# Block products of the merge gates: weight sums by accumulating DMAs, activation sums and one conditioning group in other stages

## The chip, the core and the metric

One core of a Trainium2 chip runs the whole program. The metric is the device time of one execution in microseconds; of the kernel before three executions were timed, and their median stands for it.

## The reference

Two layers of a trunk with 512 latent and 128 context tokens, which the kernel runs as one block of 640 tokens (5 tiles of 128) with 1024 channels. Cut to what matters here:

```python
def _layer(x, shift, scale, gate, w_in_l, conv_w_l, w_branch_l, w_o_l, ln_g_l, ln_b_l, attn_fn):
    h = (_layernorm(x) * (1.0 + scale) + shift).astype(x.dtype)
    q, k, v, z_a, cb, cc, cx, z_b, fx, z_c, g = jnp.split(h @ w_in_l, offsets, axis=-1)
    y_a = attn_fn(q, k, v) * jax.nn.silu(z_a)
    y_b = _short_conv(cb, cc, cx, conv_w_l) * jax.nn.silu(z_b)
    y_c = _fourier(fx) * jax.nn.silu(z_c)
    gates = jax.nn.sigmoid(g.reshape(b, s, N_BRANCH, D_MODEL))
    merged = (gates[:, :, 0] * (y_a @ w_branch_l[0]) + gates[:, :, 1] * (y_b @ w_branch_l[1])
              + gates[:, :, 2] * (y_c @ w_branch_l[2]))
    r = _layernorm(DEEPNORM_ALPHA * x + gate * (merged @ w_o_l)) * ln_g_l + ln_b_l
```

`shift`, `scale` and `gate` come from silu(cond) @ w_mod + b_mod. Everything is float32.

## The kernel before

Every matrix product is made of three matmuls: each operand is split into a high and a low part (ScalarE copies the high part, `copy`; VectorE or GpSimd subtracts for the low part), and high x high, high x low and low x high are added up in PSUM. Weights come through `Raw.load` (SP's DMA queue, 256 KB each, 6 buffers of the pool `wr`) and are split into `hl` tiles (5 buffers of `wp`). The lists of `Load(raws, steps)` in the order of the jobs set the order of loads, sums and splits; `run` emits them as far ahead as 6 raw and 5 split tiles allow, and a scheduler then orders the instructions of each engine, which run in order.

A layer goes: keys, values and queries; attention with the other projections as filler; the Fourier branch (`use_fx`, `channels`, `positions`, between the projections of `fx` and `z_c`); the gate stage; the output projection. The first layer also computes the conditioning of the second: group (1, 1) in `mod_steps` beside the Fourier stage, with loads `modf` of 256 KB, and groups (1, 2) and (1, 3) as `mod_piece`s (loads `rawm` of 512 KB, products and sums `moda` on VectorE), one after each pair of the gate stage.

The gate stage computes the 3072 gate columns. Twelve times a layer, `pair(b, m)` takes two blocks of 128 columns, cuts weights and activations in 2 x 2 blocks and uses seven block products in place of eight (`seventh`, 12 matmuls of 320 columns each). In the pair's four weight blocks a11, a12, a21, a22 and their sums, `Sum` makes the sums on VectorE (`sub`, three tiles and a scratch tile `s3`). The products are called p1 to p7 after the number given to `hl`; p1 and p2 need activations as they are, p5, p6, p7 the sums `T` made by `sums(q)` (q = 0, 1), and p4 needs `last_sum`, which overwrites a part of `act` once the last projection of the old activations is done. They add up in three PSUM banks y, x, z, drawn with the Fourier stage's g1, g2 and f1 to f3 from the four `aux` buffers. Between the products stand the branch products `pb` of the pair before (`between`), 24 matmuls each, in eight of the twelve pairs.

Of the kernel before, what the change touches and what calls it, by code (L numbers as in the profile page):

```python
# [19 lines left out]
TOK = 640  # L20
# [14 lines left out]
def body(nc, tc, I, O, ctx):  # L35
# [4 lines left out]
    big = pool("big", 1)  # L40
# [30 lines left out]
    def sub(out, a, b):  # L71
        nc.vector.tensor_tensor(out=out, in0=a, in1=b, op=ALU.subtract)  # L72
# [4 lines left out]
    def add(out, a, b):  # L77
        nc.vector.tensor_tensor(out=out, in0=a, in1=b, op=ALU.add)
# [46 lines left out]
    class Raw:  # L125
        def __init__(self, src, nm):
            self.src, self.nm, self.tile = src, nm, None
            self.stage = build_stage[0]

        def load(self):  # L130
            self.tile = wr.tile([128, 512], F32, name=f"raw{self.nm}", tag="raw")
            if self.src is not None:
                nc.sync.dma_start(out=self.tile, in_=self.src)

    class Split:
        def __init__(self, raw, nm, frees):
# [5 lines left out]
            copy(self.hl[:, 0], raw)  # L142
            eng.tensor_tensor(out=self.hl[:, 1], in0=raw, in1=fr(self.hl[:, 0]), op=ALU.subtract)  # L143

    class Sum:
        def __init__(self, out, a, b, frees=()):
            self.raws, self.frees = [out, a, b], frees

        def emit(self, eng):
            out, a, b = self.raws  # L150
            sub(out.tile, a.tile, b.tile)

    class Load:

# [26 lines left out]
    def job(body, load=None):  # L181
        jobs.append((load, body))

    def run():
        raws = [r for ld, _ in jobs if ld for r in ld.raws]
        steps = [x for ld, _ in jobs if ld for x in ld.steps]
        loaded = done = split = raw_live = hl_live = 0
        for i, (ld, bd) in enumerate(jobs):
            while i >= 3:
                if loaded < len(raws) and raws[loaded].stage <= stage[0] and raw_live < N_RAW:  # L190
                    raws[loaded].load()
                    loaded += 1
                    raw_live += 1
                    continue
                if done == len(steps):
                    break
                x = steps[done]
                if any(r.tile is None for r in x.raws):
                    break
                if isinstance(x, Sum):  # L200
                    x.emit(nc.vector)
                elif hl_live < N_HL:
                    behind = () if split == 4 or split > 7 else ("xT",) if split < 4 else ("hi", "lo")
                    with ExitStack() as st:
# [339 lines left out]
    def layer(l):  # L544
# [367 lines left out]
        def whole(out, kh, q, half):  # L912
            add(as_block(out), fr(block(kh, q, half, 0)), fr(block(kh, q, half, 1)))

        def sums(q):
            def body():
                def put(i, t):
                    hi, lo = (S["T"][i][:, z, 2 * q:2 * q + 2].rearrange("p k n -> p (k n)") for z in range(2))
                    split(hi, lo, t[:, :TOK])
                a, b, c = row(f"ta{l}{q}"), row(f"tb{l}{q}"), tmp(f"tc{l}{q}")  # L920
                whole(a, 0, q, 1)
                whole(b, 0, q, 0)
                whole(c, 1, q, 1)
                sub(b[:, :TOK], a[:, :TOK], b[:, :TOK])
                add(a[:, :TOK], c[:, :TOK], a[:, :TOK])
                add(c[:, :TOK], c[:, :TOK], b[:, :TOK])
                put(1, c)
                put(0, b)
                put(2, a)
            return body  # L930

        def last_sum():
            for q in range(2):
                a, b = row(f"td{l}{q}"), row(f"te{l}{q}")
                whole(a, 1, q, 0)
                hi, lo = (S["T"][1][:, z, 2 * q:2 * q + 2].rearrange("p k n -> p (k n)") for z in range(2))
                add(b[:, :TOK], fr(hi), fr(lo))
                sub(a[:, :TOK], a[:, :TOK], b[:, :TOK])
                split(block(0, q, 1, 0), block(0, q, 1, 1), as_block(a))

        def quarter(t, half):
            return t.rearrange("p (t h i) -> p t h i", h=2, i=64)[:, :, half]

        def pair(b, m, between=()):
            nm = f"{l}{b}{m}"
            (a11, a12), (a21, a22) = ([Raw(I["w_in"][l, C_G + b * 8 + 2 * m + i][:, h * 512:(h + 1) * 512],
                                           f"g{nm}{i}{h}") for h in range(2)] for i in range(2))
            s3 = Raw(None, f"g{nm}s")
            ps, G = {}, []

            def old(half, kh):
                return lambda k, z: act[:, :, z, 4 * kh + k, 64 * half:64 * half + 64]

            def new(i):
                return lambda k, z: S["T"][i][:, z, k]
# [27 lines left out]
            def plus(i, half):  # L983
                return lambda out: add(quarter(G[i], half), out, quarter(G[i], half))

            def sigmoid(o, i):
                nc.scalar.activation(o, i, AF.Sigmoid)

            def last_y(out):
                sigmoid(quarter(G[1], 0), out)  # L990
                sigmoid(quarter(G[1], 1), quarter(G[1], 1))

            def last_z(out):
                plus(0, 1)(out)
                sigmoid(G[0], G[0])

            def u3(out):
                keep(1, 1)(out)
                plus(1, 1)(ps["z"][:, :320].rearrange("p (t i) -> p t i", i=64))

            def hl(raw, frees, i):
                return Split(raw, f"g{nm}p{i}", frees)
            job(seventh("y", old(0, 0), True, keep(0, 0)), Load([a11, a21, a22, s3, a12], [hl(a11, [], 1)]))
            job(seventh("x", old(0, 1), True, plus(0, 0)), Load([], [hl(a12, [], 2)]))
            job(seventh("y", new(1), False, keep(0, 1)),
                Load([], [Sum(s3, a21, a11), Sum(a21, a21, a22), Sum(a11, a11, a21), hl(a11, [], 6)]))
            job(seventh("z", new(0), True, lambda out: None), Load([], [hl(a21, [a21], 5)]))
            job(seventh("y", new(2), False, u3), Load([], [hl(s3, [s3], 7)]))
            if between:
                between[0]()  # L1010
            job(seventh("y", lambda k, z: act[:, :, z, k, 64:128], False, last_y), Load([], [hl(a22, [a22], 4)]))
            job(seventh("z", old(1, 1), False, last_z), Load([], [Sum(a12, a12, a11, [a11]), hl(a12, [a12], 3)]))
            if between:
                between[1]()

        def use_p(b, c):
            def use(ps):
# [22 lines left out]
                    split(w[:, 0, 2 * q + z], w[:, 1, 2 * q + z], ld.raw(z))  # L1040
            job(body, load(I["w_o"][l, i // 2, (i % 2) * 2 + q], 2, f"o{l}{i}{q}", True))

        fm = {}

        def begin_mod():
            t = big.tile([128, 4096], F32, name="modf", tag="F")
            fm["a"] = t[:, :1024].rearrange("p (s n) -> p s n", s=2)
            fm["r"] = [t[:, 1024 + 512 * i:1536 + 512 * i] for i in range(6)]
        if l == 0:
            side.extend(mod_steps(((1, 1),), lambda: fm["a"], lambda: fm["r"]))  # L1050
            job(begin_mod)
        inproj(l, C_FX, use_fx(0))
        beside(2)
        inproj(l, C_FX + 1, use_fx(1))
        beside(2)
        for g in range(4):
            job(channels(g))
            beside(1)
            inproj(l, C_ZC + g, use_zc(g))
            if g == 3:  # L1060
                job(last_sum)
            beside(1)
            job(positions(g))
            if g < 2:
                inproj(l, C_FX + g + 2, use_fx(g + 2))
            if g == 1:
                beside(99)
                job(begin_sums)
                job(sums(0))
            if g == 2:  # L1070
                job(sums(1))

        pieces = [(1, n, kp) for n in ((2, 3) if l == 0 else (4, 5)) for kp in range(4)]

        def piece():
            if pieces:
# [240 lines left out]
```

## Time and profile before

| | us |
|---|---|
| median of 3 executions | 1269.46 |
| lowest, highest | 1268.49, 1272.26 |
| profiled execution, time | 1267.92 |
| profiled execution, span | 1266.1 |

| engine | busy, us | share of the span |
|---|---|---|
| TensorE matmul (PE) | 1226.5 | 97% |
| TensorE weight load (PEld) | 1178.1 | 93% |
| VectorE (DVE) | 950.4 | 75% |
| ScalarE (ACT) | 577.5 | 46% |
| GpSimd (POOL) | 174.1 | 14% |

The span is the time from the first to the last instruction; the time holds what lies around it as well. The page also gives the granted TensorE clock (a share of full speed) and the DMA traffic by slices of the span. The gate stage of the first layer runs from about 345 to 545 us of the span, that of the second from about 955 to 1155 us.

### The profile page before, as it was taken

To read this page: it belongs to the slowest core of one execution; us is meant where nothing else is said; L and a number is where in the kernel's file an instruction comes from. 1 tells how busy PE (TensorE), PEld (TensorE's weight loads), DVE (VectorE), ACT (ScalarE), POOL (GpSimd) and SP (SyncE) were. 2 spreads that over 40 slices of the span, in tenths; PEclk is the share of its full clock that TensorE was granted. 3 is DMA by queue.
4 is the path that set the end of the run, shared out by engine and by line. 5 is a ranking of instruction groups with operands and counts; after the bars stand their busy time and mean duration, and the time that the engine had idled before them with its cause. 6 is when DMAs were issued, how large, how long until landed. Compare 5 with 4: busy or idle time off the path is not lost.

```text
span 1266.1 us, 20852 instructions
## 1 busy us (share of the span) xinstructions
PE 1226.5 (97%) x8016; PEld 1178.1 (93%) x8016; DVE 950.4 (75%) x1710; ACT 577.5 (46%) x1113; POOL 174.1 (14%) x164
## 2 busy tenths in 40 slices
PE   6899999999989999999999999999997999999997
PEld 4699999999979999999889999999997999999986
DVE  6995686978999766678787655755579986766776
ACT  5446555554443443364244645555444444435410
POOL 3303223130000000000130233332000000000001
PEclk9999999999989999999999999999999999999999
DMA  9432132325124323234512221112312522323341
GB/s 378 170 123 68 51 104 72 100 67 175 34 85 165 100 83 102 76 121 132 222 71 72 67 68 50 60 51 76 101 39 78 177 90 84 117 60 101 116 183 50
DMA packets 61068, 131.07 MB, mean 104 GB/s; under 512 B 7144, under 2 KB 7720, under 8 KB 60712
## 3 DMA queue, kind: packets, MB, share of 16 engines
q1 hardware_dynamic: 59808, 125.35, 29.7%
q0 software_dynamic: 720, 4.10, 0.9%
q8 instruction: 63, 1.03, 0.3%
q14 instruction: 37, 0.30, 0.1%
q10 hardware_dynamic: 440, 0.30, 0.1%
HBM read 124.19 MB, written 5.52 MB: 102 GB/s over the span
## 4 chain that ended last, share of the span: by engine, by line
PE 91%; DVE 3%; DMA 3%; issue 1%; ACT 1%; POOL 0%; DVEq 0%; SPq 0%; POOLq 0%; ACTq 0%
PE y L964 13%; PE p L516 12%; PE p L518 12%; PE p L517 12%; PE z L964 6%; PE pb L516 5%; PE pb L518 5%; PE pb L517 4%; PE x L964 3%; PE o L1142 3%; PE o L1140 3%; PE o L1141 3%; PE pt L705 2%; PE s L656 2%; DMA rawm<-in_w_mod 1%; DMA raww<-in_w_in 1%
## 5 line engine op out<-in xcount | busy, mean ns | idle before, releaser
L516 PE MATMUL p<-act,hlw 128*128 128x256 f32 (+1 forms) x1024 | 321.2, 314 | 0.9 <-ACT vt L69 0.9
L518 PE MATMUL p<-act,hlw 128*128 128x256 f32 (+1 forms) x1024 | 318.4, 311 | 0.0
L517 PE MATMUL p<-act,hlw 128*128 128x256 f32 (+1 forms) x1024 | 317.4, 310 | 0.0
L516 PEld LDWEIGHTS p<-act,hlw 128*128 128x128 f32 x1024 | 193.4, 189 | 2.6 <-ACT vt L69 1.2
L517 PEld LDWEIGHTS p<-act,hlw 128*128 128x128 f32 x1024 | 192.7, 188 | 1.3
L518 PEld LDWEIGHTS p<-act,hlw 128*128 128x128 f32 x1024 | 192.7, 188 | 1.2
L687 POOL TENSOR_SCALAR P<-P,rc 128x384 f32<-128x384 f32 (+2 forms) x80 | 113.5, 1434 | 253.8 <-DVE rc L685 116.5
L69 ACT ACTIVATE hlw<-raww 128x512 fp32r<-128x512 f32 x136 | 84.8, 629 | 114.8 <-PE p L518 103.2
L143 DVE TENSOR_TENSOR hlw<-raww,hlw 128x512 fp32r<-128x512 f32 x130 | 91.3, 704 | 22.8 <-ACT hlw L69 21.1
L1140 PE MATMUL o<-wo,act 128*128 128x512 f32 (+1 forms) x168 | 63.5, 381 | 0.0
L1141 PE MATMUL o<-wo,act 128*128 128x512 f32 (+1 forms) x168 | 63.4, 379 | 0.0
L1142 PE MATMUL o<-wo,act 128*128 128x512 f32 (+1 forms) x168 | 63.3, 379 | 0.0
L312 POOL TENSOR_TENSOR rso<-rso,nhalf 128x1 f32<-128x1 f32 x10 | 14.2, 1425 | 355.6 <-DVE rso L311 355.6
L72 DVE TENSOR_TENSOR pT<-pt,pT 128x512 fp32r<-128x512 f32 x60 | 40.2, 686 | 16.2 <-ACT pT L69 16.1
L69 ACT ACTIVATE gs<-y 128x320 f32<-128x320 f32 x48 | 20.9, 435 | 68.8 <-PE y L964 65.1
L72 DVE TENSOR_TENSOR rawg<-rawg,rawg 128x512 f32<-128x512 f32 x72 | 49.5, 687 | 1.2
L69 ACT ACTIVATE pT<-pt 128x512 fp32r<-128x512 f32 x60 | 34.8, 594 | 30.9 <-PE pt L705 20.6
L143 POOL TENSOR_TENSOR hlw<-raww,hlw 128x512 fp32r<-128x512 f32 x6 | 8.5, 1425 | 260.7 <-ACT hlw L69 260.7
L659 DVE CUSTOM_DVE_ANT_0 P<-s,mask 128x384 f32<-128x384 f32 (+1 forms) x64 | 38.3, 617 | 6.1 <-PE s L656 5.9
L681 ACT ACTIVATE P<-P,nm 128x384 f32<-128x384 f32 (+1 forms) x64 | 42.1, 659 | 1.1 <-DVE es L72 0.7
L516 PE MATMUL pb<-yc,hlb 128*128 128x256 f32 (+1 forms) x128 | 40.1, 313 | 1.4 <-ACT hlb L69 1.4
L516 PE MATMUL pb<-yb,hlb 128*128 128x256 f32 (+1 forms) x128 | 40.0, 313 | 0.5 <-ACT hlb L69 0.5
(661 smaller groups left out, 2983.1 us busy)
## 6 DMA issues: line engine op xcount, KB each, us to landing
raww<-in_w_in SPq DMA_DIRECT2D x136, 256.0 KB, 2.9
rawg<-in_w_in SPq DMA_DIRECT2D x96, 256.0 KB, 3.0
rawm<-in_w_mod SPq DMA_DIRECT2D x32, 512.0 KB, 5.0
rawb<-in_w_branch SPq DMA_DIRECT2D x48, 256.0 KB, 2.8
rawo<-in_w_o SPq DMA_DIRECT2D x32, 256.0 KB, 3.1
sz<-in_w_mod SPq DMA_DIRECT2D x24, 256.0 KB, 2.9
dft<-in_dft POOLq DMA_DIRECT2D x2, 1542.0 KB, 7.3
x<-in_x SPq DMA_DIRECT2D x5, 512.0 KB, 6.1
```

What stands on the lines that cost most here:

```text
L69: nc.scalar.activation(out, in_, AF.Copy)
L72: nc.vector.tensor_tensor(out=out, in0=a, in1=b, op=ALU.subtract)
L143: eng.tensor_tensor(out=self.hl[:, 1], in0=raw, in1=fr(self.hl[:, 0]), op=ALU.subtract)
L516: nc.tensor.matmul(ps[:, a:b], lhsT=ld.w(0, k), rhs=mh, start=k == 0, stop=False)
L517: nc.tensor.matmul(ps[:, a:b], lhsT=ld.w(0, k), rhs=ml, start=False, stop=False)
L518: nc.tensor.matmul(ps[:, a:b], lhsT=ld.w(1, k), rhs=mh, start=False, stop=k == nk - 1)
L681: nc.scalar.activation(P[:, g, :W], srcs[g], AF.Exp, scale=0.125, bias=nm_[:, g:g + 1], accum_out=sm[:, g:g + 1])
L687: nc.gpsimd.tensor_scalar(out=P[:, g, :W], in0=P[:, g, :W], scalar1=rc[:, g:g + 1], scalar2=None, op0=ALU.mult)
L964: nc.tensor.matmul(out, lhsT=ld.w(z, k), rhs=moving(k, y), start=first and k == i == 0, stop=k == 3 and i == 2, skip_group_check=True)
L1140: nc.tensor.matmul(ps, lhsT=act[:, t, 0, k], rhs=w[:, 0], start=k == 0, stop=False)
L1141: nc.tensor.matmul(ps, lhsT=act[:, t, 0, k], rhs=w[:, 1], start=False, stop=False)
L1142: nc.tensor.matmul(ps, lhsT=act[:, t, 1, k], rhs=w[:, 0], start=False, stop=k == NK - 1)
```

## The change

1. The weight sums of a pair are made by DMAs that add their source to the tile they write (`Acc`, issued from GpSimd's queue): a21 += a22, a11 += a21 and a21 += a11 read the second operand from HBM again, a12 += a21 reads the tile. The signs of the seven products are turned so that only plus signs are left in the weights; the activation sums (`sums`, `last_sum`) and the sigmoids take the signs. `s3` is gone.
2. The order of the seven products is p1, p2, p5, p6, p7, p4, p3 (before p1, p2, p6, p5, p7, p4, p3), and the branch products stand after p5 and after p4.
3. `sums(0)` stands after the first `fx` projection and `sums(1)` after the first `positions`, in both layers. Before, `sums(0)` stood after `positions(1)` and `sums(1)` after `positions(2)`.
4. In the first layer conditioning group (1, 1) is no longer done beside the Fourier stage, but as four more pieces of the gate stage: twelve in place of eight.

```diff
-    class Sum:
-        def __init__(self, out, a, b, frees=()):
-            self.raws, self.frees = [out, a, b], frees
+    class Acc:
+        def __init__(self, out, src, frees=()):
+            self.out, self.src, self.frees = out, src, frees
+            self.raws = [out] + ([src] if isinstance(src, Raw) else [])

         def emit(self, eng):
-            out, a, b = self.raws
-            sub(out.tile, a.tile, b.tile)
+            src = self.src.tile if isinstance(self.src, Raw) else self.src
+            nc.gpsimd.dma_start(out=self.out.tile, in_=src, accum_op=ALU.add)
...
-                sub(b[:, :TOK], a[:, :TOK], b[:, :TOK])
-                add(a[:, :TOK], c[:, :TOK], a[:, :TOK])
-                add(c[:, :TOK], c[:, :TOK], b[:, :TOK])
+                sub(b[:, :TOK], b[:, :TOK], a[:, :TOK])
+                sub(a[:, :TOK], c[:, :TOK], a[:, :TOK])
+                minus(c[:, :TOK], c[:, :TOK], b[:, :TOK])
...
-                sub(a[:, :TOK], a[:, :TOK], b[:, :TOK])
+                minus(a[:, :TOK], b[:, :TOK], a[:, :TOK])
...
-            job(seventh("y", old(0, 0), True, keep(0, 0)), Load([a11, a21, a22, s3, a12], [hl(a11, [], 1)]))
-            job(seventh("x", old(0, 1), True, plus(0, 0)), Load([], [hl(a12, [], 2)]))
-            job(seventh("y", new(1), False, keep(0, 1)),
-                Load([], [Sum(s3, a21, a11), Sum(a21, a21, a22), Sum(a11, a11, a21), hl(a11, [], 6)]))
-            job(seventh("z", new(0), True, lambda out: None), Load([], [hl(a21, [a21], 5)]))
-            job(seventh("y", new(2), False, u3), Load([], [hl(s3, [s3], 7)]))
+            job(seventh("y", old(0, 0), True, keep(0, 0)), Load([a11, a12, a21], [hl(a11, [], 1), Acc(a21, srcs[1][1])]))
+            job(seventh("x", old(0, 1), True, plus(0, 0)), Load([a22], [Acc(a11, srcs[1][0]), hl(a12, [], 2)]))
+            job(seventh("z", new(0), True, lambda out: None), Load([], [hl(a21, [], 5), Acc(a21, srcs[0][0])]))
             if between:
                 between[0]()
+            job(seventh("y", new(1), False, keep(0, 1)), Load([], [hl(a21, [], 6), Acc(a12, a21, [a21])]))
+            job(seventh("y", new(2), False, third_y), Load([], [hl(a11, [a11], 7)]))
             job(seventh("y", lambda k, z: act[:, :, z, k, 64:128], False, last_y), Load([], [hl(a22, [a22], 4)]))
-            job(seventh("z", old(1, 1), False, last_z), Load([], [Sum(a12, a12, a11, [a11]), hl(a12, [a12], 3)]))
             if between:
                 between[1]()
+            job(seventh("z", old(1, 1), False, last_z), Load([], [hl(a12, [a12], 3)]))
...
-        if l == 0:
-            side.extend(mod_steps(((1, 1),), lambda: fm["a"], lambda: fm["r"]))
-            job(begin_mod)
         inproj(l, C_FX, use_fx(0))
-        beside(2)
+        job(begin_sums)
+        job(sums(0))
         inproj(l, C_FX + 1, use_fx(1))
...
             job(positions(g))
+            if g == 0:
+                job(sums(1))
             if g < 2:
                 inproj(l, C_FX + g + 2, use_fx(g + 2))
-            if g == 1:
-                beside(99)
-                job(begin_sums)
-                job(sums(0))
-            if g == 2:
-                job(sums(1))
...
-        pieces = [(1, n, kp) for n in ((2, 3) if l == 0 else (4, 5)) for kp in range(4)]
+        pieces = [(1, n, kp) for n in ((1, 2, 3) if l == 0 else (4, 5)) for kp in range(4)]
```

VectorE at the opening of the second layer's gate stage, around the product of the last `z_c` projection (`sgzc13`). `ta11`, `tb11` and `tc11` are rows of `sums(1)`, `tb1` and `tf1` the tiles `T`, `td` and `te` rows of `last_sum`. Before:

```order
L75 TENSOR_TENSOR sgzc13_10078<-p1_33_10029,sgzc13_10078 128x640
L143 TENSOR_TENSOR hlg110p7_10086<-rawg110s_9752,hlg110p7_10086 128x512
L72 TENSOR_TENSOR tb11_9990<-ta11_9989,tb11_9990 128x640
L72 TENSOR_TENSOR yc1_9344<-sgzc12_9947,yc1_9344 128x640
L143 TENSOR_TENSOR hlg110p4_10151<-rawg11011_9670,hlg110p4_10151 128x512
L78 TENSOR_TENSOR ta11_9989<-tc11_9991,ta11_9989 128x640
L78 TENSOR_TENSOR te10_10092<-tb1_9856 128x640
L72 TENSOR_TENSOR tb1_9856<-tb11_9990,tb1_9856 128x640
L143 TENSOR_TENSOR hlg110p3_10172<-rawg11001_9756,hlg110p3_10172 128x512
L78 TENSOR_TENSOR tc11_9991<-tc11_9991,tb11_9990 128x640
L72 TENSOR_TENSOR td10_10091<-td10_10091,te10_10092 128x640
L72 TENSOR_TENSOR tf1_9857<-ta11_9989,tf1_9857 128x640
```

The same place now:

```order
L75 TENSOR_TENSOR sgzc13_10067<-p1_33_10018,sgzc13_10067 128x640
L142 TENSOR_TENSOR hlg110p7_10076<-rawg11000_9575,hlg110p7_10076 128x512
L918 SCALAR_TENSOR_TENSOR td10_10081<-te10_10082,td10_10081 128x640
L235 TENSOR_SCALAR moda14_10256<-rawm140_10257,scond_100 128x512 x2
L918 SCALAR_TENSOR_TENSOR td11_10088<-te11_10089,td11_10088 128x640
L142 TENSOR_TENSOR hlg110p4_10141<-rawg11011_9772,hlg110p4_10141 128x512
L238 SCALAR_TENSOR_TENSOR moda14_10256<-rawm140_10257,scond_100,moda14_10256 128x512 x2
L72 TENSOR_TENSOR act_109<-td10_10081,act_109 128x5x2x64
L78 TENSOR_TENSOR fy13_10115<-g213_10096,fy13_10115 128x256
```

The rows of `sums(1)` have left this place, and `last_sum` (`td`) and the reading of g2 (`fy13`) follow the last projection more closely.

GpSimd's queue in the first layer, from the Fourier stage on (`ff`: rows of the Fourier branch; raw tiles end in 00 for a11, 01 for a12, 10 for a21; `rawg010..` is the first pair, `rawg011..` the second). Before:

```order
L805 DMA dft0_3042<-in_dft 128x3084
L818 COPY ff01_3178<-fx01_3176 128x128
L817 COPY ff01_3178<-fx01_3176 128x2
L818 COPY ff02_3374<-fx02_3372 128x128
L817 COPY ff02_3374<-fx02_3372 128x2
L818 COPY ff03_3575<-fx03_3573 128x128
L817 COPY ff03_3575<-fx03_3573 128x2
```

Now, up to the second pair:

```order
L153 DMA rawg01010_3402<-in_w_in 128x512
L819 COPY ff02_3385<-fx02_3383 128x2
L820 COPY ff03_3572<-fx03_3570 128x128
L819 COPY ff03_3572<-fx03_3570 128x2
L153 DMA rawg01000_3287<-in_w_in 128x512
L153 DMA rawg01010_3402<-in_w_in 128x512
L153 DMA rawg01001_3397<-rawg01010_3402 128x512
L153 DMA rawg01110_3786<-in_w_in 128x512
L153 DMA rawg01100_3489<-in_w_in 128x512
L153 DMA rawg01110_3786<-in_w_in 128x512
L153 DMA rawg01101_3584<-rawg01110_3786 128x512
```

Four accumulations of each pair stand in one row on this queue, and nothing else stands between them to the end of the stage.

ScalarE in the third pair of the first layer (`hlg012p5` is the split of p5, and so on; `gs` are evacuations and sigmoids of gates). Now:

```order
L69 ACTIVATE hlg012p2_4099<-rawg01201_3966 128x512
L69 ACTIVATE hlg012p5_4116<-rawg01210_3996 128x512
L69 ACTIVATE hlb0_1_2_0_4146<-rawb0_1_2_0_4033 128x512
L69 ACTIVATE gs0120_4190<-y012_4177 128x5x64
L991 ACTIVATE gs0111_3991<-y011_3977 128x5x64
L991 ACTIVATE gs0111_3991<-gs0111_3991 128x5x64
L69 ACTIVATE hlg012p6_4165<-rawg01210_3996 128x512
L69 ACTIVATE hlg012p7_4193<-rawg01200_3946 128x512
```

Before, the row of p6 read a11's tile and came ahead of p5's; now both read a21's tile (`rawg01210`), and p6's copy follows p5's by four instructions with an accumulation into that tile between them.

## Rows read from the trace of the kernel before

**Rows 1.** The page, part 1: busy time of the engines.
```profile
PE 1226.5 (97%) x8016; PEld 1178.1 (93%) x8016; DVE 950.4 (75%) x1710; ACT 577.5 (46%) x1113; POOL 174.1 (14%) x164
```
**Rows 2.** Windows: length; busy (count) PE, PEld, DVE, ACT, POOL; clock; DMA share; GB/s.
```profile
0.00:50.00 50.00, 38.89 (x246) 27.92 (x247) 39.07 (x68) 29.65 (x46) 22.39 (x24) 1.00 0.80 306
400.00:450.00 50.00, 50.00 (x343) 50.00 (x342) 39.20 (x66) 18.45 (x36) 0.00 (x0) 1.00 0.31 100
900.00:950.00 50.00, 50.00 (x353) 49.17 (x352) 32.73 (x60) 20.89 (x42) 2.44 (x6) 1.00 0.16 48
...
345.00:350.00 5.00, 2.91 (x19) 2.56 (x19) 4.90 (x11) 1.88 (x5) 0.00 (x0) 0.96 0.15 52
350.00:355.00 5.00, 3.90 (x14) 3.16 (x15) 5.00 (x9) 1.75 (x3) 0.00 (x0) 0.50 0.15 52
355.00:360.00 5.00, 5.00 (x22) 5.00 (x21) 5.00 (x8) 2.51 (x4) 0.00 (x0) 0.52 0.09 17
360.00:365.00 5.00, 3.73 (x26) 3.47 (x25) 5.00 (x11) 2.25 (x6) 0.00 (x0) 1.00 0.66 250
365.00:370.00 5.00, 4.05 (x25) 3.49 (x24) 5.00 (x9) 2.38 (x6) 0.00 (x0) 1.00 0.29 105
960.00:965.00 5.00, 2.69 (x20) 2.42 (x18) 4.16 (x7) 2.52 (x4) 0.00 (x0) 1.00 0.70 211
965.00:970.00 5.00, 2.26 (x8) 2.26 (x9) 5.00 (x8) 2.47 (x6) 0.00 (x0) 0.74 0.29 106
970.00:975.00 5.00, 3.42 (x19) 2.93 (x18) 5.00 (x11) 1.95 (x5) 0.00 (x0) 0.92 0.00 0
```
**Rows 3.** Waits of PE, 300 to 420 us and 930 to 1010 us: total, times, longest.
```profile
PE g L869 <- DVE al L72: 2.1, 1, 2.1
PE z L964 <- ACT fy L69: 1.3, 1, 1.3
PE z L964 <- ACT fy L69: 5.1, 1, 5.1
```
**Rows 4.** Groups of DVE's instructions, 285 to 345 us; the last row is the page's.
```profile
L236 DVE SCALAR_TENSOR_TENSOR modf<-modf,scond 128x512 f32<-128x512 f32 x14 | 10.1, 745 | 1.3 <-DMA modf<-in_w_mod 1.3
L78 DVE TENSOR_TENSOR tc<-act 128x640 f32<-128x640 f32 x2 | 1.6, 816 | 0.0
L72 DVE TENSOR_TENSOR rawg<-rawg,rawg 128x512 f32<-128x512 f32 x72 | 49.5, 687 | 1.2
```
**Rows 5.** The chain that ended last: the x product of two neighbouring pairs.
```profile
434.38 1.76 PE x L964 x12
453.78 1.76 PE x L964 x12
```
**Rows 6.** Timeline, ACT and DVE: a split, and ACT's copy that frees g1.
```profile
343.42 0.63 ACT L69 ACTIVATE hlg010p<-rawg 128x512 fp32r<-128x512 f32 x1 [1.53 <-PE p L518]
344.08 0.69 DVE L143 TENSOR_TENSOR hlg010p<-rawg,hlg010p 128x512 fp32r<-128x512 f32 x1 [0.76 <-ACT hlg010p L69]
966.29 0.74 ACT L69 ACTIVATE act<-td 128x640 fp32r<-128x640 f32 x1
967.03 0.66 ACT L69 ACTIVATE fy<-g 128x257 f32<-128x257 f32 x2
```
**Rows 7.** DMA issues: bytes each, median us from issue to landing.
```profile
rawg<-in_w_in SPq DMA_DIRECT2D x96, 256.0 KB, 3.0
dft<-in_dft POOLq DMA_DIRECT2D x2, 1542.0 KB, 7.3
trig<-in_trig POOLq DMA_DIRECT2D x1, 384.0 KB, 3.4
mask<-in_mask POOLq DMA_DIRECT2D x1, 192.0 KB, 2.6
```
**Rows 8.** Timeline: a DMA issue on POOL and DVE's work beside it.
```profile
46.78 0.54 POOL L112 DMA_DIRECT2D mask<-in_mask  x1
46.64 0.81 DVE L508 TENSOR_TENSOR act<-xT,act 128x640 fp32r<-128x640 f32 x1
```

More of the change, by code (lines that the diff above doesn't have):

```diff
@@ L131, in load @@
             self.tile = wr.tile([128, 512], F32, name=f"raw{self.nm}", tag="raw")
-            if self.src is not None:
-                nc.sync.dma_start(out=self.tile, in_=self.src)
+            nc.sync.dma_start(out=self.tile, in_=self.src)
     class Split:
@@ L199, in run @@
                     break
-                if isinstance(x, Sum):
-                    x.emit(nc.vector)
+                if isinstance(x, Acc):
+                    x.emit(nc.gpsimd)
                 elif hl_live < N_HL:
@@ L913, in whole, with minus @@
             add(as_block(out), fr(block(kh, q, half, 0)), fr(block(kh, q, half, 1)))
+        def minus(out, a, b):
+            nc.vector.scalar_tensor_tensor(out=out, in0=a, scalar=-1.0, in1=b, op0=ALU.mult, op1=ALU.subtract)
         def sums(q):
@@ L945, in pair @@
             nm = f"{l}{b}{m}"
-            (a11, a12), (a21, a22) = ([Raw(I["w_in"][l, C_G + b * 8 + 2 * m + i][:, h * 512:(h + 1) * 512],
-                                           f"g{nm}{i}{h}") for h in range(2)] for i in range(2))
-            s3 = Raw(None, f"g{nm}s")
+            srcs = [[I["w_in"][l, C_G + b * 8 + 2 * m + i][:, h * 512:(h + 1) * 512] for h in range(2)] for i in range(2)]
+            (a11, a12), (a21, a22) = ([Raw(srcs[i][h], f"g{nm}{i}{h}") for h in range(2)] for i in range(2))
             ps, G = {}, []
@@ L984, in plus, with sigmoid @@
                 return lambda out: add(quarter(G[i], half), out, quarter(G[i], half))
-            def sigmoid(o, i):
-                nc.scalar.activation(o, i, AF.Sigmoid)
+            def sigmoid(o, i, scale=1.0):
+                nc.scalar.activation(o, i, AF.Sigmoid, scale=scale)
             def last_y(out):
-                sigmoid(quarter(G[1], 0), out)
-                sigmoid(quarter(G[1], 1), quarter(G[1], 1))
+                sigmoid(quarter(G[1], 0), out, -1.0)
+                sigmoid(quarter(G[1], 1), quarter(G[1], 1), -1.0)
             def last_z(out):
@@ L995, in last_z, with third_y @@
                 sigmoid(G[0], G[0])
-            def u3(out):
+            def third_y(out):
                 keep(1, 1)(out)
@@ L1041, in load_wo @@
             job(body, load(I["w_o"][l, i // 2, (i % 2) * 2 + q], 2, f"o{l}{i}{q}", True))
[L1043 to L1048, printed above, removed]
-        if l == 0:
-            side.extend(mod_steps(((1, 1),), lambda: fm["a"], lambda: fm["r"]))
-            job(begin_mod)
         inproj(l, C_FX, use_fx(0))
-        beside(2)
+        job(begin_sums)
+        job(sums(0))
         inproj(l, C_FX + 1, use_fx(1))
-        beside(2)
         for g in range(4):
             job(channels(g))
-            beside(1)
             inproj(l, C_ZC + g, use_zc(g))
@@ L1061, in layer @@
                 job(last_sum)
-            beside(1)
             job(positions(g))
+            if g == 0:
+                job(sums(1))
             if g < 2:
                 inproj(l, C_FX + g + 2, use_fx(g + 2))
-            if g == 1:
-                beside(99)
-                job(begin_sums)
-                job(sums(0))
-            if g == 2:
-                job(sums(1))
-        pieces = [(1, n, kp) for n in ((2, 3) if l == 0 else (4, 5)) for kp in range(4)]
+        pieces = [(1, n, kp) for n in ((1, 2, 3) if l == 0 else (4, 5)) for kp in range(4)]
         def piece():
```

## The prediction

> **What bounds the kernel now.** I read the page's busy times first, then the windows, then PE's waits, and last the instructions of VectorE where PE waits. PE is busy 1226.5 of 1266.1 us [rows 1], and in the middle of the gate stage all of 50 us, with VectorE at 39.2 [rows 2]. There a faster VectorE or a leaner load is worth nothing, since no matmul is removed: the change has seven products of 12 matmuls in a pair as before. What it can give back lies in the two openings of the gate stage. From 345 to 370 us and from 960 to 975 us PE stands still for part of every window but one and runs for some time at half clock (0.50, that is 1.2 in place of 2.4 GHz, after a window with 2.1 us of idle time), while VectorE is busy nearly without a gap [rows 2]. The waits name the way: positions(3) waits for VectorE's `al`; the z product waits 1.3 and 5.1 us for ScalarE's `fy`, which frees the PSUM buffer of g1 [rows 3], and ScalarE's copy of `act` ahead of it had waited for VectorE's `td` [rows 6].
>
> The price of an opening is read per 5 us window as idle time plus busy time x (1 - clock) [rows 2]. First layer: 2.09 + 0.12, then 1.10 + 1.95, 2.40, 1.27 and 0.95: 9.9 us. Second layer: 2.31, then 2.74 + 0.59, 1.58 + 0.27: 7.5 us. Together 17.4 us, the most that the change can return by this way.
>
> **The change, part by part.**
>
> *Weight sums off VectorE.* A pair loses four instructions of 0.69 us (72 of them in the row; the 24 that write `s3` are of the same shape) [rows 4]: 2.7 us of VectorE in each of 24 pairs. In the steady stage that is worth nothing (PE is full); in an opening, where the sums of the first two pairs fall in, it is 5.5 us of a full engine.
>
> *Activation sums earlier.* `sums(1)` is nine instructions of 640 columns at 0.82 us [rows 4], 7.3 us. They leave the opening, and `sums(0)` moves ahead by as much. In the second layer VectorE was busy 32.7 of the 50 us ahead of the gate stage [rows 2], so the two fit in 17 us of room. In the first layer room comes from the next part. `last_sum` stays where it was, eight instructions, since it needs the last projection done.
>
> *Conditioning group (1, 1).* Beside the Fourier stage of the first layer 14 instructions of 0.745 us go [rows 4], 10.4 us, and two of the same kind that open the group; they come back as four pieces in the last four pairs, which have lost 4 x 2.7 = 11 us of sums. Eight loads of 256 KB on SP become four of 512 KB. I put this at nothing: it is hidden behind PE in both places. If VectorE were short there, it would cost what it takes there, some 2.6 us a pair.
>
> An opening thus loses some 7.3 + 5.5 = 13 us of VectorE's work out of the 25 to 30 us in which it had no gap, and `td`, `fy` and `al` come nearly as soon as their inputs. What is late next is ScalarE's order. z needs g1's buffer: after y's end ScalarE does the split of p4, which waits for y's weights (0.63), the copy of `act` (0.74) and `fy` (0.66), together 2.0 us [rows 6], while PE has only x (12 matmuls, 1.76 us [rows 5]). With hand-overs I put 0.8 us there, 0.4 and 0.7 us at the two evacuations of y that stand in the same queue, and 0.5 us at positions(3): 2.4 us a layer, 4.8 in all. Gaps of about 1 us, as from 360 to 370 us, left the clock at 1.00 in the trace [rows 2].
>
> *Accumulating DMAs.* This is the unknown price. No accumulation is in the trace. From below: a plain DMA issued from GpSimd lands in 2.6 us for 192 KB and in 3.4 for 384 KB [rows 7], so 2.9 us for 256 KB. From above: 7.3 us, the row of 1542 KB, six times the bytes [rows 7]. An accumulation moves its tile twice (read and written back); by the two ends of these rows, 4.7 us for 1350 KB, a second 256 KB adds 0.9 us, so 3.8. I take **X = 4.2 us** with 0.4 us for meeting SP's loads, near the lower end since the bytes are nearer to those rows; both ends go into the range.
>
> The DMAs stand in a ring: a21 is loaded (3.0 us [rows 7]), a22 is added (X), the sum is split for p5 (0.63 and 0.69 us, 1.35 from start to end [rows 6]), a11 is added (X), the result is added to a12 (X), and only then is the buffer free for a load of the next pair; behind that load SP's queue holds all later loads, and behind the wait GpSimd's queue holds the later accumulations. With 0.6 us for four hand-overs a turn takes 3X + 5.0 = 17.6 us. A pair takes 19.4 us, the distance of two x products [rows 5]. So the ring is covered, with 1.8 us to spare in a turn and once 7.0 - 1.35 = 5.6 us, since a split can start four products ahead of its use. Limit without loss: 3X + 5.0 = 19.4 + 5.6/7, X = 5.1 us. The three last pairs have no branch products and take 12.3 us, but there the chain from p5's to p6's split has five products (8.8 us) to run: 1.35 + X + 1.35 plus hand-overs, X up to 5 to 5.5 us. Bandwidth is no bound: four accumulations of 256 KB in 19.4 us are 54 GB/s in and as much out on top of 100, and 306 were moved in the first 50 us [rows 2]. For new small waits of this kind I add 1.0 us.
>
> The signs (`minus`, the scale of the sigmoid) and the order of the products change no count of instructions: nothing, and in the middle of the stage PE hides them.
>
> **The sum.** 17.4 - 4.8 - 1.0 = 11.6 us less. Against the profiled execution (1267.9 us, a span of 1266.1 and 1.8 around it) that is 1256.3; the profiled execution is 1.5 us below the median of the runs, 1269.5, from which the forecast is **1257.9 us**. Its own range is 1251 (all 17.4 and the 1.0 us by which the runs spread downwards) to 1263 (half returned).
>
> **A rule against the change.** The row shows a DMA issue on GpSimd of 0.54 us while VectorE ran a two-input tensor_tensor of 0.81 us that began earlier and ended later [rows 8]: it wasn't held off. The Trainium skill (SBUF — State Buffer, Summary: rules for kernel authors) advises against hiding a GpSimd-issued DMA under VectorE's work, as descriptor generation is starved while VectorE is in its 2x or 4x mode. The row agrees only so far as it had no such mode to meet; that the gate stage has none, no run here shows. If issues were held off, rival C would follow.
>
> **The rivals.**
>
> A, *the accumulations are slow* and the ring becomes the bound: slower than before. Take X = 5.75, the middle between 4.2 and 7.3. A turn takes 22.25 us, 2.85 more than a pair; over seven turns 20, less the 5.6 in reserve 14.4, and 0.75 for each of the last three pairs, 2.2: 16.6 us a layer, 33.2 in two, less 11.6: 1269.5 + 21.6 = **1291 us**. It decides from X = 5.3 on, where the loss equals the gain. For it: the upper row, and that ScalarE and VectorE run in order, so that a late sum holds up what stands behind its split. Against it: the plain DMAs, all within 0.4 us of 3.
>
> B, *the opening stays shut*: the stall isn't VectorE's load but the hand-over of PSUM buffers through ScalarE's order, and moved sums hold up the Fourier stage instead. For it: 5.1 us of the second layer's 7.5 are the wait for `fy`. Against it: that copy stood behind `act`, which waited for VectorE. It gives back some 3 us: **1266 us**, within what can be told from no change.
>
> C, *GpSimd's issues are held off* by VectorE, by two instructions of 0.69 us each [rows 4]: X = 5.6, a turn of 21.8; (2.4 x 7 - 5.6 + 3 x 0.6) x 2 = 26 less 11.6: **1284 us**. Against it: rows 8.
>
> **How the numbers follow.** Forecast 0.65, A 0.17, B 0.14, C 0.04. A measurement of this kernel tells some 0.3% (3.8 us) from no change. Faster by more: nearly all of the forecast and a third of B, 0.67. Within: the rest of B, and A near its turning point, 0.11. Slower: A and C, 0.22. The range of 8 in 10 runs from 1251 to 1284: it takes in B, C and A up to X near 5.6 and leaves out the longer half of A and a few hundredths below.
>
> **What would show it.** Right: in both openings PE without idle windows of 2 us, clock at 1.00, VectorE with gaps there; `al`, `fy` no longer among PE's long waits; accumulations landing in 4 to 5 us; x products still 19.4 us apart. Wrong: x products more than 20 us apart, PE waiting for splits whose copies waited for a DMA on GpSimd's queue, landings over 5.3 us (A, or C if the issue itself is long); or the same waits for `fy` as before (B).

## The result, and the profile after

The changed kernel takes 1284.07 us (median of 4 runs, 1282.2 to 1285.17), the kernel before beside it 1268.97: a ratio of 1.011, 95% interval 1.0092 to 1.0128. It is 15 us slower; the forecast was 1257.9 us, the range ended at 1284. The profiled execution has a span of 1280.4 us, 14.3 more than before.

The page of the changed kernel, parts 1, 5 and 6 (to be read with [rows 1, 7]):

```profile
PE 1231.2 (96%) x8016; PEld 1177.4 (92%) x8016; DVE 889.9 (69%) x1614; ACT 572.2 (45%) x1113; POOL 259.6 (20%) x260
...
L153 POOL DMA_DIRECT2D rawg<-in_w_in x72 | 63.3, 916 | 289.3 <-DMA rawg<-in_w_in 58.3
...
L153 POOL DMA_DIRECT2D rawg<-rawg x24 | 20.7, 864 | 103.9 <-DMA rawg<-in_w_in 66.0
...
rawg<-in_w_in SPq DMA_DIRECT2D x96, 256.0 KB, 3.4
...
rawg<-in_w_in POOLq DMA_DIRECT2D x72, 256.0 KB, 4.9
...
rawg<-rawg POOLq DMA_DIRECT2D x24, 256.0 KB, 3.5
```

VectorE has 60 us less to do, and TensorE stands still for 49 us of the span, where it was 40; it is also busy 4.7 us longer with the same 8016 matmuls. An accumulation lands 4.9 us after its issue when it reads HBM and 3.5 us when it reads a tile.

The windows of the openings (columns as in [rows 2]):

```profile
345.00:350.00 5.00, 5.00 (x37) 4.72 (x36) 5.00 (x8) 1.22 (x2) 0.04 (x1) 1.00 0.47 110
350.00:355.00 5.00, 4.87 (x33) 4.61 (x32) 4.62 (x9) 3.44 (x8) 0.87 (x1) 1.00 0.81 206
355.00:360.00 5.00, 4.11 (x28) 3.76 (x27) 5.00 (x10) 1.70 (x3) 0.24 (x1) 1.00 0.63 213
...
965.00:970.00 5.00, 5.00 (x36) 4.72 (x36) 4.54 (x9) 2.00 (x4) 0.85 (x1) 1.00 0.47 156
970.00:975.00 5.00, 4.87 (x33) 4.46 (x31) 5.00 (x10) 3.34 (x9) 0.00 (x0) 1.00 0.90 250
```

Against [rows 2] the holes are gone and the granted clock is 1.00 (2.4 GHz) throughout; the long waits for `al` and `fy` of [rows 3] don't appear. So the openings opened, and the loss lies behind them. The x product, one in each pair, shows where. PE's timeline, its rows in the first layer's fifth and sixth pair, the second layer's, and the second layer's last three pairs, then those last three in the kernel before:

```profile
425.19 0.46 PE L968 MATMUL x<-act,hlg020p 128*128 128x320 f32 x2
...
446.37 0.46 PE L968 MATMUL x<-act,hlg021p 128*128 128x320 f32 x2
...
1040.82 0.46 PE L968 MATMUL x<-act,hlg120p 128*128 128x320 f32 x2
...
1060.22 0.46 PE L968 MATMUL x<-act,hlg121p 128*128 128x320 f32 x2
...
1137.38 1.92 PE L968 MATMUL x<-act,hlg101p 128*128 128x320 f32 x12
...
1152.79 1.92 PE L968 MATMUL x<-act,hlg102p 128*128 128x320 f32 x12
...
1170.19 1.92 PE L968 MATMUL x<-act,hlg103p 128*128 128x320 f32 x12
```
```profile
1136.35 1.92 PE L964 MATMUL x<-act,hlg101p 128*128 128x320 f32 x12
...
1147.20 0.46 PE L964 MATMUL x<-act,hlg102p 128*128 128x320 f32 x2
...
1160.99 1.78 PE L964 MATMUL x<-act,hlg103p 128*128 128x320 f32 x11
```

Pairs with branch products are some 21 us apart in the first layer (20.5 to 21.7), 19.4 in the second, as before [rows 5]; the last pairs are 15.4 and 17.4 us apart, where they were 10.9 and 13.8. From the starts of these rows, in every run below, the gate stage is cut in three: first to fourth x (the opening), fourth to ninth (branch pairs), ninth to the output projection (the last pairs and what follows). First layer / second layer, us:

| kernel | first x, layer 1 | 1st to 4th | 4th to 9th | 9th to projection | median |
|---|---|---|---|---|---|
| before | 358.6 | 56.1 / 60.0 | 97.4 / 97.4 | 67.7 / 67.7 | 1268.97 |
| changed | 351.3 | 52.6 / 52.2 | 105.5 / 99.2 | 79.0 / 79.5 | 1284.07 |
| all sums on VectorE | 351.4 | 52.0 / 52.0 | 102.3 / 100.7 | 66.5 / 66.4 | 1254.61 |
| a21 loaded first | 351.4 | 51.0 / 51.0 | 100.4 / 99.2 | 75.9 / 75.0 | 1269.02 |
| a12 += a21 on VectorE | 351.8 | 51.0 / 53.8 | 99.2 / 99.2 | 71.0 / 71.7 | 1261.53 |
| the last two together | 352.5 | 51.0 / 53.3 | 99.2 / 99.2 | 68.7 / 69.8 | 1257.81 |

Changed against before: 7.3 + 3.5 + 7.7 = 18.5 us returned by the openings, 8.1 + 1.8 lost in the branch pairs and 11.2 + 11.7 behind the ninth x: 14.3 us in all, the difference of the spans. (In a run below that keeps only the signs and the new order of the products, the last column is 66.4 / 66.4, 1.3 us shorter than before, and the step from the eighth to the ninth x 1.8 us longer.)

### The profile page after: what moved, and what is told of

Its sections match the earlier page's. It is cut to its first block, busy times and chain, and to the rows that moved or that the text cites. A ratio compares the mean times of both kernels' runs of the same rounds, so it can differ in the third digit from the quotient of the medians.

```text
span 1280.4 us, 21139 instructions
## 1 busy us (share of the span) xinstructions
PE 1231.2 (96%) x8016; PEld 1177.4 (92%) x8016; DVE 889.9 (69%) x1614; ACT 572.2 (45%) x1113; POOL 259.6 (20%) x260
## 5 line engine op out<-in xcount | busy, mean ns | idle before, releaser
L153 POOL DMA_DIRECT2D rawg<-in_w_in x72 | 63.3, 916 | 289.3 <-DMA rawg<-in_w_in 58.3
L238 DVE SCALAR_TENSOR_TENSOR moda<-rawm,scond,moda 128x512 f32<-128x512 f32 x70 | 50.9, 744 | 1.0 <-DMA rawm<-in_w_mod 0.8
L72 DVE TENSOR_TENSOR pT<-pt,pT 128x512 fp32r<-128x512 f32 x60 | 40.1, 685 | 16.2 <-ACT pT L69 16.1
L518 PE MATMUL pb<-ya,hlb 128*128 128x256 f32 (+1 forms) x128 | 41.3, 323 | 3.8 <-ACT hlb L69 3.8
L153 POOL DMA_DIRECT2D rawg<-rawg x24 | 20.7, 864 | 103.9 <-DMA rawg<-in_w_in 66.0
```

Source lines behind the costliest of these rows:

```text
L153: nc.gpsimd.dma_start(out=self.out.tile, in_=src, accum_op=ALU.add)
L238: nc.vector.scalar_tensor_tensor(out=acc[:, c], in0=w, scalar=scond[:, k, c:c + 1], in1=acc[:, c], op0=ALU.mult, op1=ALU.add)
L518: nc.tensor.matmul(ps[:, a:b], lhsT=ld.w(0, k), rhs=mh, start=k == 0, stop=False)
```

## The experiments

Each was timed beside the kernel before, whose median lay between 1269.3 and 1270.3 us.

**The accumulations taken out.** Line for line in `pair`, a11 taking the sum for p7 so that no scratch tile is needed, and a22 loaded earlier, since VectorE reads its tile:

```diff
-Load([a11, a12, a21], [hl(a11, [], 1), Acc(a21, srcs[1][1])])
-Load([a22], [Acc(a11, srcs[1][0]), hl(a12, [], 2)])
-Load([], [hl(a21, [], 5), Acc(a21, srcs[0][0])])
-Load([], [hl(a21, [], 6), Acc(a12, a21, [a21])])
+Load([a11, a21, a22, a12], [hl(a11, [], 1)])
+Load([], [hl(a12, [], 2), Sum(a11, a11, a21), Sum(a21, a21, a22)])
+Load([], [hl(a21, [], 5), Sum(a21, a11, a22)])
+Load([], [hl(a21, [], 6), Sum(a12, a12, a21, [a21])])
```

> The changed kernel with all four weight sums of a pair back on VectorE (plus signs, written in place, no scratch tile); order of the products, moved activation sums and conditioning pieces as in the changed kernel. Theory L (late sums: the accumulations are the whole loss, some 30 us, and the openings' gain of 15 us hangs mostly on the moved activation sums): branch pairs back at 19.4 us, pairs without branch products at 12 to 13 us, 1252 to 1261 us. Rival P (the new order of the products or the place of the branch products makes the pairs longer): 1275 to 1285 us, pairs without branch products still at 16 us or more. Rival C (four more conditioning pieces in the first layer take VectorE and SP's queue): second layer's pairs back at 19.4 and 12 to 13 us, the first layer's branch pairs still near 21, 1262 to 1270 us. Rival S (the gain of the openings comes from the sums having left VectorE): openings as long as in the kernel before, 1266 to 1270 us.

1254.61 us, ratio 0.9884 (0.9869 to 0.9899). The last pairs are 12.3 and 12.5 us apart, and all that was lost behind the ninth x is back. The accumulations cost 29.5 us (1284.07 - 1254.61); P and S fall. The openings are as short as with accumulations, so the load that these took off VectorE wasn't needed there. The first layer's branch pairs leave some 3 us for C (102.3 against 99.2 in the best run).

The same for `b == 0` alone, the last four pairs of a layer:

> The changed kernel with the weight sums on VectorE in the last four pairs of each layer alone, which hold one or no branch product between them; the other eight accumulate by DMA as before. Theory L: the 22 us that these eight pairs lose come back, the first layer's branch pairs stay 9 us too long: 1260 to 1266 us. Rivals P and C (not the accumulations make the last pairs long): 1278 to 1285 us.

1256.4 us, ratio 0.9891 (0.9874 to 0.9908): 28 us less than the changed kernel, more than the 22 of the theory and below its range. The last column goes to 66.5 / 66.4; the first layer's branch pairs keep 103.0 us.

Only the fourth sum, `Sum(a12, a12, a21, [a21])`, in all pairs:

> The changed kernel with one accumulation of four, a12 += a21, done by VectorE; the other three stay DMAs. Theory L: the ring is shorter by 3.5 to 4 us less 0.7, so the branch pairs of the first layer come back to 19.4 us (9 us), and in the last pairs p3's split comes 3 us earlier, while p6's still waits some 4 us for its sum, so about half of their 22 us comes back: 1258 to 1270 us. If only the chain from p5's split to p6's counts: the last pairs unchanged, 1272 to 1277 us. If the accumulations are no part of the loss: 1284 us.

1261.53 us, ratio 0.9935 (0.9921 to 0.9948), as the theory had it: branch pairs 99.2, last column 71.0 / 71.7.

Accumulations with the activation sums and the conditioning group at their old places:

> The changed kernel with the activation sums and conditioning group (1, 1) at the places of the kernel before: the accumulations, signs and order of the products alone. Theory L with a loss that adds up: the kernel before plus 24 to 30 us, 1293 to 1299 us, less up to 5 us if the four sums of two pairs that left VectorE shorten the openings: 1288 to 1299. Rival C (the added conditioning pieces make the loss): 1265 to 1278 us.

1289.16 us, ratio 1.0156 (1.0139 to 1.0173), at the lower end of L. As the whole loss C falls; the first layer's fifth to eighth x, though, are 19.4 to 19.6 us apart, as in the kernel before.

**Where they hold the kernel up.** The timeline of the changed kernel, second layer, two of the last pairs (`hlg102p` are splits of the second-to-last pair):

```profile
1144.93 0.33 SPq L132 DMA_DIRECT2D rawg<-in_w_in  x1
...
1148.36 0.85 POOL L153 DMA_DIRECT2D rawg<-in_w_in  x1 [4.10 <-DVE hlg101p L142]
...
1154.51 0.63 ACT L69 ACTIVATE hlg102p<-rawg 128x512 fp32r<-128x512 f32 x1 [4.99 <-DMA rawg<-in_w_in]
...
1156.22 0.85 POOL L153 DMA_DIRECT2D rawg<-in_w_in  x1 [5.62 <-DVE hlg102p L142]
...
1160.19 1.16 ACT L69 ACTIVATE hlg102p<-rawg 128x512 fp32r<-128x512 f32 x2 [3.37 <-DMA rawg<-in_w_in]
...
1160.52 0.85 POOL L153 DMA_DIRECT2D rawg<-rawg  x1 [3.44 <-DMA rawg<-in_w_in]
...
1162.18 0.33 SPq L132 DMA_DIRECT2D rawg<-in_w_in  x1
...
1164.30 0.63 ACT L69 ACTIVATE hlg102p<-rawg 128x512 fp32r<-128x512 f32 x1 [2.11 <-DMA rawg<-rawg]
...
1165.46 0.61 ACT L69 ACTIVATE hlg103p<-rawg 128x512 fp32r<-128x512 f32 x1
...
1166.13 0.57 PE L968 MATMUL y<-act,hlg103p 128*128 128x320 f32 x2 [2.79 <-ACT hlg103p L69]
...
1166.16 0.86 POOL L153 DMA_DIRECT2D rawg<-in_w_in  x1 [4.79 <-DVE hlg102p L142]
...
1166.85 1.74 PE L968 MATMUL y<-act,hlg103p 128*128 128x320 f32 x10 [0.16 <-DVE hlg103p L142]
```

There are two chains in it. The ring: a21 is loaded (1144.93), a22 added (1148.36), the sum split for p5 (1154.51), a11 added (1156.22), p6 and p7 split (1160.19), and then the next pair's a21 is loaded (1162.18) into the buffer of a11, which p7's split has just released: six buffers go round in order, four to a pair. A turn takes 17.3 us. (The sum at 1148.36 is put down to VectorE; by its time, 0.6 us after the load lands, it waited for the load, as at 1166.16. It lands after 6.1 us, with a11 += a21 issued 1.4 us behind it and landing after 6.0; the sum at 1156.22, which stands alone, lands after 3.9.) The other: a12 += a21 (1160.52) can start only when the sum for p6 has landed, p3's split on ScalarE waits for it (1164.30), the next pair's p1 split stands behind (1165.46), and PE waits 2.79 us for that.

Each step pays its whole landing. The Trainium skill (DMA: Bandwidth & Descriptors, Two DMAs through the same engine are not ordered) says that a dependent DMA has to wait for the completion of the one before, and that one queue is no substitute; the rows agree: from the accumulation at 1156.22 to the one that reads its result, 4.3 us.

To tell the ring from the second chain:

```diff
-Load([a11, a12, a21], [hl(a11, [], 1), Acc(a21, srcs[1][1])])
+Load([a21, a11, a12], [Acc(a21, srcs[1][1]), hl(a11, [], 1)])
```

> The changed kernel with the loads of a pair in the order a21, a11, a12, a22 (changed: a11, a12, a21, a22) and a21 += a22 issued ahead of p1's split; all four sums stay accumulating DMAs. The six raw buffers go round in order, so in the changed kernel a pair's a21 is loaded into the buffer of the pair before's a11, which is free only after p7's split, and that stands on ScalarE behind p6's, which waits for two accumulations; here a21 takes a buffer that is free a pair earlier. Theory R (this ring of load, sum, split, sum, split and release, 17 to 18 us a turn, is what lasts too long in pairs of 12.3 us): the x products of the last four pairs 12.3 to 14 us apart in place of 15.4 to 17.4, the first layer's branch pairs near 19.4: 1257 to 1268 us. Theory K (inside each pair the path from p5's split through an accumulation of 4 to 5 us to p6's split is too long, whatever buffer it stands in): distances and time as in the changed kernel, 1278 to 1286 us.

1269.02 us, ratio 0.9999 (0.9988 to 1.001): 15 us back with the same DMAs, between the two forecasts. The branch pairs come back (first layer 105.5 to 100.4), as R says. The last pairs stay 16 us apart, as K says. Timeline of this kernel at the same pair:

```profile
1144.96 0.63 ACT L69 ACTIVATE hlg102p<-rawg 128x512 fp32r<-128x512 f32 x1 [2.98 <-PE y L968]
...
1146.67 0.85 POOL L153 DMA_DIRECT2D rawg<-in_w_in  x1 [0.99 <-DVE hlg102p L142]
...
1150.91 1.15 ACT L69 ACTIVATE hlg102p<-rawg 128x512 fp32r<-128x512 f32 x2 [2.72 <-DMA rawg<-in_w_in]
...
1151.48 0.87 POOL L153 DMA_DIRECT2D rawg<-rawg  x1 [3.96 <-issue]
...
1155.66 0.63 ACT L69 ACTIVATE hlg102p<-rawg 128x512 fp32r<-128x512 f32 x1 [2.75 <-DMA rawg<-rawg]
...
1156.82 0.61 ACT L69 ACTIVATE hlg103p<-rawg 128x512 fp32r<-128x512 f32 x1
...
1157.49 0.56 PE L968 MATMUL y<-act,hlg103p 128*128 128x320 f32 x2 [2.01 <-ACT hlg103p L69]
...
1158.21 2.88 PE L968 MATMUL y<-act,hlg103p 128*128 128x320 f32 x10 [0.16 <-DVE hlg103p L142]
...
1161.13 0.63 ACT L69 ACTIVATE hlg103p<-rawg 128x512 fp32r<-128x512 f32 x1 [2.85 <-PE y L968]
```

The sum of p6 (1146.67 to 1150.91) and the sum of p3 (1151.48 to 1155.66) stand one behind the other, and then the next p1's split. By the trace, the next p5's split (1161.13) waits for the p1 product, and so the second chain closes to a turn of its own: 16.2 us from p5's split (1144.96) to the next. A part of it is the clock: the p1 product runs behind PE's wait, its last ten matmuls take 2.88 us where 1.74 were enough in the changed kernel at 1166.85, and the granted clock is 0.84 and 0.82 in the windows from 1155 to 1165 us, a mean of the two levels. Two runs on this chain, the first with `Sum(a12, a12, a21, [a21])` added to the new load order:

> a21 loaded first, and a12 += a21 by VectorE; the other three sums accumulating DMAs in all pairs. Theory K2 (in the last pairs p3's split waits on ScalarE for the sum a12 += a21, which can only start when the sum for p6 has landed, and the next pair's p1 split stands behind it, so that two accumulations lie in a row in each pair of 16 to 17 us): without the second one a pair takes 16.5 less 4.1 plus 0.7, 12.5 to 13.5 us, the last four pairs to the output projection 67 to 70 us in place of 75.5: 1269 less 11 to 17, 1252 to 1258 us. Theory K1 (the one accumulation between p5's split and p6's is enough to make the pair long): 15 us and more a pair, 1264 to 1269 us.

1257.81 us, ratio 0.9904 (0.989 to 0.9918); the last pairs are 12.7 and 14.3, 14.1 and 14.1 us apart, the last column 68.7 / 69.8. K2 holds for the larger part; 13.8 us in the mean against 12.4 with all sums on VectorE leave 1.4 us a pair, which may be K1's; that was not tried by itself. The second:

```diff
+            if late:
+                late.pop()()
...
-            job(seventh("z", old(1, 1), False, last_z), Load([], [hl(a12, [a12], 3)]))
+            late.append(lambda: job(seventh("z", old(1, 1), False, last_z), Load([], [hl(a12, [a12], 3)])))
```

> a21 loaded first, all four sums accumulating DMAs, and p3 of a pair put behind p1 of the next, so that on ScalarE the next p1's split stands ahead of p3's split and not behind it. No sum, load or product is added or taken away. Theory K2: the late sum of p3 holds up nothing that the next p1 needs; the x products of the last pairs 12.3 to 14 us apart in place of 16 to 16.7: 1269 less 8 to 16, 1253 to 1261 us. Theory K1, or if p2's and p5's splits behind p3's matter as much: 15 us and more, 1264 to 1270 us.

1280.93 us, ratio 1.009 (1.0076 to 1.0104): the time misses both forecasts. The last pairs are 14.4 and 13.8, 14.4 and 14.0 us apart, some 2.2 us less than without the edit and at the upper end of what K2 says, and the last column is 73.4 / 72.1; but two new waits stand in the first layer (PE's waits, 390 to 480 us, and ScalarE's row before the first):

```profile
PE y L970 <- ACT hlg013p L69: 4.6, 1, 4.6
PE y L970 <- ACT hlg020p L69: 4.4, 1, 4.4
```
```profile
397.28 0.63 ACT L69 ACTIVATE hlg013p<-rawg 128x512 fp32r<-128x512 f32 x1 [7.00 <-DMA rawg<-in_w_in]
```

The next p1's split now waits 7 us for the load of its a11. That a12's buffer, released one product later, holds up the loads behind it was not tried by itself.

**The gain.** Three runs with all weight sums on VectorE. The conditioning group back beside the Fourier stage, four steps after each of the first two `fx` projections, `sums(0)` after the second:

> All weight sums on VectorE, and conditioning group (1, 1) of the first layer back beside the Fourier stage, ahead of the first activation sums, which wait for its buffer there and so stand one projection later. Theory L (VectorE is full in the first layer's opening because of the twelve pieces): the third to sixth pair of the first layer come down from 61.4 to 58 to 59 us, nothing is lost in the Fourier stage: 1250 to 1253 us. If the group held up the Fourier stage or the sums there: 1255 to 1264 us.

1266.5 us, ratio 0.9978 (0.9967 to 0.9989), above both forecasts. PE's waits, 290 to 420 us, name a wait that the edit itself made:

```profile
PE modq L257 <- DVE modg L253: 8.4, 1, 8.4
```

With eight steps that close together the group's last matmul holds up PE, so this run doesn't price the group in its old, loose order. From the first to the ninth x it takes 153.8 us against 154.3 with the pieces in the gate stage, but not in the same places: the opening 56.4 against 52.0, the branch pairs 97.4 against 102.3. Then signs and order alone, and the same with the group moved:

> All weight sums on VectorE, activation sums and conditioning group at the places of the kernel before: of the change only the signs, the new order of the products and the place of the branch products are left. Theory L (the moved activation sums are what opens the openings, some 12 us): 1264 to 1268 us, the last four pairs 1.3 us a layer shorter than before, the openings as before. If the order of the products opens them: 1254 to 1260 us.

> All weight sums on VectorE and the conditioning group among the pieces of the gate stage as in the changed kernel, but the activation sums back at their places of the kernel before. In the second layer nothing but the sums differs from the run with all sums on VectorE. Theory L1 (the moved activation sums alone open both openings): as with the order alone, 1268 to 1273 us, first x product of the first layer near 358 us. Theory L2 (the sums open the second layer's, 7 to 9 us, and in the first layer the group's leaving the Fourier stage does it): first x product of the first layer at 351 to 354 us, 1260 to 1266 us.

1272.13 us, ratio 1.0026 (1.0016 to 1.0035), and 1272.38 us, ratio 1.0025 (1.0016 to 1.0035). In the second, first to fourth x takes 59.8 / 59.1 us, PE waits for `fy` as before [rows 3] (280 to 420 us, and the same row from 930 to 1010 us), and PE stands still in the window 355 to 360 us, as it did in its neighbours before [rows 2], with VectorE full:

```profile
PE z L976 <- ACT fy L69: 4.3, 1, 4.3
```
```profile
355.00:360.00 5.00, 1.50 (x11) 1.24 (x9) 5.00 (x8) 2.60 (x4) 0.00 (x0) 1.00 0.74 258
```

The moved activation sums alone are worth 1272.38 - 1254.61 = 17.8 us, and moving the group is worth nothing in sum without them. L1 holds by the time; by the first x product of the first layer it doesn't, since that stands at 354.5 us, close to where L2 had it, and not near 358. So the group's leaving does bring the first x forward, by 4.0 us (358.5 with signs and order alone), and the pieces take it back: opening 57.6 to 59.8, branch pairs 97.4 to 100.8. Signs and order cost 2.9 us; the three columns add up to 221.4 and 225.1 us (before: 221.2 and 225.1), and in the profiled executions the difference lies between the first layer's output projection and the second layer's first x, 384.3 us against 381.0. It wasn't followed up.

**Versions that beat both.** a12 += a21 on VectorE in all pairs and all four sums there in the last four pairs; and the same with a21 loaded first:

> a12 += a21 by VectorE in all pairs, the other three sums by VectorE too in the last four pairs of a layer, by accumulating DMAs in the first eight. Theory R: the branch pairs as in the run with the third sum on VectorE, the last pairs as in the run with them on VectorE: 1261.5 less 10 us, 1248 to 1254 us, so below both. If what VectorE saves in the branch pairs is worth nothing: as with all sums on VectorE, 1254 to 1257 us.

> a21 loaded first; in the first eight pairs of a layer three sums by accumulating DMAs and a12 += a21 by VectorE, in the last four all by VectorE. Theory R: the second layer's pairs lose the 2.6 us that they still lose without the new load order (22.0 + 21.4 + 17.6 us in place of 19.4 three times), the rest as there: 1252.1 less 2 to 3, 1249 to 1251 us. If the order of the loads is worth nothing with three DMAs: 1251 to 1254 us.

1252.09 us, ratio 0.987 (0.9855 to 0.9886), and 1252.59 us, ratio 0.9863 (0.9846 to 0.988). The first came as expected. The second misses theory R's forecast and lies in the other's: with three accumulations the order of the loads is worth nothing measurable, and the second layer's opening stays at 53.2 us. The plain version with all sums on VectorE is 2 to 2.5 us behind, within the spread of these runs.

## Why the prediction was wrong

- *Openings.* Right in mechanism, undersized: 17.4 us priced, 4.8 kept back for ScalarE's order, 12.6 expected; 18.5 came back in the profile, more than the 17.4 that was called the most, and 17.8 by the two runs that differ only in the place of the sums. Nothing of the 0.8 us at `fy` is among PE's long waits. Rival B falls.
- *Weight sums off VectorE,* 5.5 us of a full engine in an opening: worth nothing there once the activation sums have moved (52.6 / 52.2 in the changed kernel, 52.0 / 52.0 with the weight sums on VectorE).
- *Conditioning pieces "in the last four pairs", put at nothing.* They don't run there: the scheduler draws them ahead, and their `moda` rows stand between 350.1 and 426.4 us in the first layer. The group's move measures nothing in sum (1272.13 and 1272.38), but it isn't hidden behind PE in both places: it gives 4.0 us ahead of the first x and takes 2.2 and 3.4 in the opening and the branch pairs.
- *X = 4.2 us.* Right in size: 4.9 (three of four) and 3.5, a mean of 4.55. A's turning point of 5.3 was wrong, since the kernel lost at a smaller X.
- *The ring,* 17.6 us a turn through a21's buffer with three accumulations. Measured 17.3 in the last pairs, but by another way: two accumulations, since the next a21 takes a11's buffer. In the second layer the branch pairs hide all of it (19.4); in the first they lose some 6 us against the best run. Both a21 first (100.4) and a12 += a21 on VectorE with the old order of loads (99.2) bring them back, so it isn't shown that the ring alone binds there. With the conditioning group and the activation sums at their old places, and all sums accumulating, these pairs are 19.4 us apart again; which of the two parts lengthens them was not tried alone. Accumulations land in 5.1 us there and 4.7 in the second layer (DMA issues, 380 to 480 and 1000 to 1100 us):

```profile
rawg<-in_w_in POOLq DMA_DIRECT2D x13, 256.0 KB, 5.1
...
rawg<-in_w_in POOLq DMA_DIRECT2D x15, 256.0 KB, 4.7
```

- **The step that failed:** "The three last pairs have no branch products and take 12.3 us, but there the chain from p5's to p6's split has five products (8.8 us) to run", good for an X up to 5 to 5.5. That link held: in the changed kernel it runs from 1154.51 to 1160.19, 5.7 us. But these pairs cost 12.5 and 13.1 us a layer against sums on VectorE, 25.6 of the 27.5 us between the two profiled spans (1280.4 and 1252.9). I set a single link of the chain against the pair in place of the whole turn. The forecast's own turn, 17.6 us, was longer than these pairs by 5.3, and a reserve of 5.6 us covers one of them: 3 x 5.3 less 5.6 is 10 us a layer, 20 in all, and with it the sum would have been 1278 us. The runs part the loss further. Of the 12.5 and 13.1 us, 9.4 and 8.6 are left with a21 loaded first, 4.5 and 5.3 with a12 += a21 on VectorE, 2.2 and 3.3 with both. So the larger part is the second chain, which the sum didn't have: the sum of p3 behind the sum of p6 and ahead of the next p1 on ScalarE.
- *Rival A* has the mechanism (late sums hold up what stands behind their split) but the wrong place: it counted 0.75 us for each last pair. *Rival C* named 1284 us, by chance: the 96 issues take 0.87 us in the median in place of the 0.54 of [rows 8], the longest 1.33, less as a whole than the 1.4 us that C adds to each, and GpSimd is idle between them. ("Slower: A and C, 0.22" is more than the 0.21 that the two have together.)

## What to carry to other kernels

Set the whole turn of a chain of loads, sums and releases against the shortest period in which it has to run, not against the usual one, and follow each buffer in the order in which the pool hands them out: which tile a load takes decides what it waits for. A sum that moves from an engine to a DMA gets longer (0.69 to 4.9 us here), so it may go where its turn has room and not where two stand in a row ahead of work that runs in order. When a change has several parts, time them apart: here one gave 17.8 us and another took 29.5.

## What was not expected

An accumulation costs the DMA engines about twice a load, by the page's part 3 of the changed kernel and of the kernel before (packets, MB, share of 16 engines):

```profile
q1 hardware_dynamic: 59232, 125.35, 29.7%
q0 software_dynamic: 14544, 29.27, 13.0%
```
```profile
q0 software_dynamic: 720, 4.10, 0.9%
```

GpSimd's queue (q0) held only a few loads before; the accumulations add 25.17 MB and 12.1% of the span to it, 0.48% per MB, where the loads of SP's queue (q1) take 0.24%. A source in a tile landed sooner than one in HBM here, 3.5 against 4.9 us for the same 256 KB.
